# Two low-rank projections computed with one shared stationary operand for the high and low weight parts

## The chip, the core and the metric

The kernel runs on one core of a Trainium2 chip. The metric is device time in microseconds (us) for one execution. A core has five engines that run side by side, each with its own instruction order: TensorE (PE, the matrix multiplier, with a separate line for loading its stationary operand), VectorE (DVE), ScalarE (ACT), GpSimd (POOL) and SyncE (SP, which mostly issues DMAs). They wait for each other through semaphores. Matmul results go to PSUM banks and are emptied from there by ACT or DVE.

A matmul has a stationary operand (up to 128 rows by 128 columns, the weights here) and a moving operand (the same rows by 512 columns here: 512 positions of the sequence). Its sum runs over the rows.

## The reference, cut to what matters

The program is one layer of a decoder: a norm, one input projection, an RWKV-7 branch and an S5 branch, their gated merge, an output projection, and a gated MLP with a short convolution. The input is 1024 positions by 1024 channels, in float32. The change concerns two lines of the RWKV branch:

```python
p = token_shift(h @ w_in[:, :1792], mu)
r, k, v, wd, ad, gd = split(p, ...)            # 512, 512, 512, 64, 64, 128 columns
w = -softplus(-(w0 + tanh(wd) @ w2)) - 0.5     # w2: 64 x 512
a = sigmoid(a0 + ad @ a2)                      # a2: 64 x 512
g = sigmoid(gd) @ g2                           # g2: 128 x 512, this one is not changed
```

`tanh(wd) @ w2` and `ad @ a2` are the two low-rank projections: each sums over only 64 values and gives 512 channels for each of the 1024 positions.

## The kernel before, in words

**Precision.** PE multiplies in a reduced format (fp32r). Each float32 operand is therefore split into a high part, which is a cast to that format, and a low part, which is what the cast lost. A product is then three matmuls that add up in one PSUM bank: high weights by high data, high weights by low data, low weights by high data. `mm3_steps` (L161) issues these as L172, L173 and L174, and `split` (L225) makes the two parts of data: a cast on ACT (L226) and a subtraction on DVE (L227). `load_w` (L142) does the same for weights: a DMA into a tile `wf` of which there are two buffers (L155), a cast to `wh` on ACT (L156), a subtraction to `wl` on DVE (L157).

**Layout.** Data lie transposed, with channels on the 128 partitions and positions along the row, in two halves of 512 positions (`th` 0 and 1). One output tile is 128 channels by 512 positions, which is one PSUM bank. Tiles of the projections are named `gm`; there are four such banks while the S5 stage runs, two in the RWKV stage.

**The two projections.** The input projection's tile 12 holds `wd` in its rows 0 to 63 and `ad` in rows 64 to 127. `shifted` (L1078) empties it with the token shift (L1083 on ACT, then L1084 and L1086 or L1088 on DVE), `shifted_into` applies tanh to rows 0 to 63 (L1098) and splits the whole tile into two `lx` tiles (L1101, which calls L226 and L227). `lowrank` (L1106) then loads `w_lr[0]`, which is w2 in rows 0 to 63 and zeros below, does 8 outputs (2 halves of the sequence by 4 tiles of channels) with `mm3_steps`, and does the same with `w_lr[1]`, zeros in rows 0 to 63 and a2 below. Both thus multiply all 128 rows, and the zeros drop the half that does not belong. Each output goes through ACT (L1119, for w2 also L1121) to memory (L1122). `lowrank` is called once more for g2, further on.

**The order of the work.** Instructions are put in order when the program is built. `drive` (L185) is a planner with a clock of its own, `self.now`. It has *lanes*, which are generators of a stage's main work (in the first stage, which I call the S5 stage, the S5 scan and its tables; in the second, the RWKV stage, preparation, chain and output), and a *background list*, `self.fill`, of projections that may be put between them. Each step of a lane says how long it takes and how long its result needs; while no lane is ready, or the lanes have used up their credit, the planner takes the next step of the background list and advances its clock by that step's count, 0.68 for three matmuls. How far the background list has come when a lane's step is placed therefore depends on these counts.

The background list begins with `mix_in` (L1133): tile 12, then the tiles of r, k and v (`rkv`) for a quarter of the channels, mixed with the two low-rank projections: `mixed(a, b, 3)` puts one step of `b` behind every three of `a`. Then come tile 13, further r, k and v, the gates (`gate_tiles`), later the merge (`merge`, evicted at L1203 on DVE) and the output projection. In the RWKV stage the list supplies PE with work while the lanes wait for DVE. Names that occur there are: `cz` (L715) and L723, two products of the preparation; L784 to L812, the triangular inverse's work on DVE; L822, small matmuls of 32 rows that combine the inverses' blocks; L879, matmuls of 64 rows in the chain; L935, the transposes of the stage's output. At the end of each stage a *drain* does what is left of the list or of a part of it.

**Elsewhere.** `s5_setup` and what follows it (L439 to L512) makes tables on DVE while the projections begin. Behind the RWKV stage comes the MLP (from about 735 us of the span to the end), which the change does not touch.

## Time and profile before

| | |
|---|---|
| three runs | 1462.29, 1463.06, 1465.25 us, median 1463.06 |
| the profiled execution | 1461.26 us |
| its span, first to last instruction | 1459.5 us |
| granted TensorE clock, mean | 0.986 of full |
| PE busy | 1402.2 us, 96% of the span |
| DVE busy | 1087.5 us, 75% |
| ACT busy | 746.7 us, 51% |
| the two projections' evictions (L1119) | first at 78.5, last at 122.5 us |

The span in six stretches. The columns are the stretch and its length in us, then busy time of PE, PE's weight load, DVE, ACT and POOL with the number of instructions, the granted clock, the share of the DMA engines and GB/s. The first is the front, the second has the projections beside the S5 tables, the third S5 and the first half of the RWKV stage, the fourth is the middle of the RWKV stage, the fifth its end, the sixth the MLP.

```profile
0.00:80.00 80.00, 66.42 (x281) 52.08 (x282) 71.92 (x239) 56.35 (x90) 1.18 (x10) 0.98 0.59 174
80.00:280.00 200.00, 198.95 (x1047) 167.46 (x1045) 137.87 (x198) 129.54 (x228) 6.27 (x21) 1.00 0.43 137
280.00:515.00 235.00, 230.96 (x2664) 184.12 (x2665) 147.90 (x292) 106.54 (x221) 3.60 (x10) 0.99 0.39 127
515.00:600.00 85.00, 69.86 (x452) 55.93 (x451) 74.08 (x149) 52.87 (x95) 1.08 (x2) 0.91 0.58 174
600.00:735.00 135.00, 132.42 (x1580) 103.84 (x1579) 85.50 (x165) 60.62 (x116) 4.27 (x8) 0.99 0.39 125
735.00:1460.00 725.00, 703.62 (x3142) 579.51 (x3140) 570.25 (x744) 340.82 (x449) 18.50 (x29) 0.99 0.42 137
```

In a row of a timeline, as the prediction shows them, stand the start in us, the recorded duration, the engine, the line and operation, output and inputs by their names in the program, the tile of PE's array for a matmul, shapes, and the number of instructions taken together. A bracket gives how long the engine stood idle before the row and which engine's instruction ended that. Matmuls overlap in the records: what one costs is the distance from start to start, not the duration.

### The profile page before, as it was taken

To read this page: it belongs to the slowest core of one execution; us is meant where nothing else is said; L and a number is where in the kernel's file an instruction comes from. 1 tells how busy PE (TensorE), PEld (TensorE's weight loads), DVE (VectorE), ACT (ScalarE), POOL (GpSimd) and SP (SyncE) were. 2 spreads that over 40 slices of the span, in tenths; PEclk is the share of its full clock that TensorE was granted. 3 is DMA by queue.
4 is the path that set the end of the run, shared out by engine and by line. 5 is a ranking of instruction groups with operands and counts; after the bars stand their busy time and mean duration, and the time that the engine had idled before them with its cause. 6 is when DMAs were issued, how large, how long until landed. Compare 5 with 4: busy or idle time off the path is not lost. (4 is left out here: it accounts for less than half of the span.)

```text
span 1459.5 us, 23887 instructions
## 1 busy us (share of the span) xinstructions
PE 1402.2 (96%) x9156; PEld 1142.9 (78%) x9156; DVE 1087.5 (75%) x1783; ACT 746.7 (51%) x1197; POOL 34.9 (2%) x80
## 2 busy tenths in 40 slices
PE   7999999999999989899999999999999999999996
PEld 5778888878878767678788887888888887888785
DVE  8986886378327788548688898777777777597677
ACT  7667775453424564535455464454544445444451
POOL 0000000000000000000000000000000000000001
PEclk9999999999999999899999999999999999999998
DMA  7454433542413565433555543222222228934723
GB/s 221 116 190 128 144 117 108 188 146 80 139 60 110 162 193 165 138 111 116 172 195 180 158 133 122 87 83 76 75 84 87 87 73 273 328 112 144 239 79 115
DMA packets 119682, 202.04 MB, mean 138 GB/s; under 512 B 28672, under 2 KB 34944, under 8 KB 119568
## 3 DMA queue, kind: packets, MB, share of 16 engines
q1 hardware_dynamic: 113296, 182.43, 39.4%
q0 software_dynamic: 4544, 15.80, 2.9%
q10 hardware_dynamic: 1728, 2.29, 0.4%
q8 instruction: 72, 1.18, 0.3%
q14 instruction: 42, 0.34, 0.1%
HBM read 148.04 MB, written 50.33 MB: 136 GB/s over the span
## 5 line engine op out<-in xcount | busy, mean ns | idle before, releaser
L172 PE MATMUL gm<-hh,wh 128*128 128x512 f32 x672 | 276.2, 411 | 9.1 <-DVE hl L1203 4.6
L173 PE MATMUL gm<-hl,wh 128*128 128x512 f32 x672 | 264.8, 394 | 0.0
L174 PE MATMUL gm<-hh,wl 128*128 128x512 f32 x672 | 264.6, 394 | 0.0
L156 ACT CAST wh<-wf 128x512 fp32r<-128x512 f32 x171 | 105.2, 618 | 140.9 <-PE gm L173 72.5
L157 DVE TENSOR_TENSOR wl<-wf,wh 128x512 fp32r<-128x512 f32 x171 | 117.2, 688 | 76.2 <-ACT wh L156 75.6
L172 PEld LDWEIGHTS gm<-hh,wh 128*128 128x128 f32 x672 | 127.5, 190 | 41.5 <-DVE hl L1203 5.7
L174 PEld LDWEIGHTS gm<-hh,wl 128*128 128x128 f32 x672 | 127.7, 190 | 27.8
L173 PEld LDWEIGHTS gm<-hl,wh 128*128 128x128 f32 x672 | 127.8, 190 | 24.7 <-issue 1.0
L1626 PE MATMUL d<-xl,wh 128*128 128x512 f32 x308 | 120.7, 392 | 2.1 <-DVE xl L227 2.0
L1625 PE MATMUL d<-xh,wh 128*128 128x512 f32 x308 | 120.8, 392 | 2.1 <-ACT xh L226 2.1
L1627 PE MATMUL d<-xh,wl 128*128 128x512 f32 x308 | 120.6, 392 | 0.0
L1451 PE MATMUL rp<-t,h 128*128 128x512 f32 x216 | 84.4, 391 | 1.5 <-ACT p L1465 1.5
L1453 PE MATMUL rp<-t,l 128*128 128x512 f32 x216 | 84.2, 390 | 0.5 <-DVE l L227 0.5
L1452 PE MATMUL rp<-t,h 128*128 128x512 f32 x216 | 84.1, 389 | 0.0
L1626 PEld LDWEIGHTS d<-xl,wh 128*128 128x128 f32 x308 | 58.2, 189 | 15.5 <-DVE xl L227 3.4
L1625 PEld LDWEIGHTS d<-xh,wh 128*128 128x128 f32 x308 | 58.2, 189 | 14.6 <-ACT xh L226 2.4
L1627 PEld LDWEIGHTS d<-xh,wl 128*128 128x128 f32 x308 | 58.1, 189 | 12.0
L226 ACT CAST h<-r 128x1024 fp32r<-128x1024 f32 x34 | 35.8, 1054 | 61.1 <-PE rp L1452 29.6
L227 DVE TENSOR_TENSOR l<-r,h 128x1024 fp32r<-128x1024 f32 x34 | 41.6, 1225 | 29.2 <-ACT h L226 27.7
L1472 DVE SCALAR_TENSOR_TENSOR y<-zv,vecs,y 128x1023 f32<-128x1023 f32 (+1 forms) x36 | 46.1, 1281 | 8.5 <-ACT y L1470 8.5
L1465 ACT COPY p<-rp 128x512 f32<-128x512 f32 x54 | 31.0, 574 | 36.6 <-PE rp L1453 36.6
L1451 PEld LDWEIGHTS rp<-t,h 128*128 128x128 f32 x216 | 40.5, 188 | 11.1 <-ACT p L1465 2.4
(459 smaller groups left out, 3127.6 us busy)
## 6 DMA issues: line engine op xcount, KB each, us to landing
r<-in_w_up_dram SPq DMA_DIRECT2D x36, 512.0 KB, 3.6
wf<-in_w_in_dram SPq DMA_DIRECT2D x62, 256.0 KB, 3.0
st<-in_w_down_dram SPq DMA_DIRECT2D x55, 256.0 KB, 4.0
st<-ACT SPq DMA_DIRECT2D x44, 256.0 KB, 4.3
wf<-in_w_up_dram SPq DMA_DIRECT2D x36, 256.0 KB, 2.9
ACT<-y POOLq DMA_DIRECT2D x18, 512.0 KB, 2.9
GT<-ev SPq DMA_DIRECT2D x32, 256.0 KB, 2.5
wf<-in_w_br_dram SPq DMA_DIRECT2D x32, 256.0 KB, 2.6
```

What stands on the lines that cost most here:

```text
L156: nc.scalar.copy(h[:, :n], f[:, :n])
L157: nc.vector.tensor_tensor(l[:, :n], f[:, :n], h[:, :n].bitcast(F32), ALU.subtract)
L172: mm(ps, a, xh[k], start=k == 0, stop=False)
L173: mm(ps, a, xl[k], start=False, stop=False)
L174: mm(ps, b, xh[k], start=False, stop=k == n - 1)
L1451: mm(ps, wh[:, c], xh, start=first and k == 0, stop=False, skip_group_check=True)
L1452: mm(ps, wh[:, c], xl, start=False, stop=False, skip_group_check=True)
L1453: mm(ps, wl[:, c], xh, start=False, stop=k == 3, skip_group_check=True)
L1472: V.scalar_tensor_tensor(y[:, lag:], z[:, 0:1024 - lag], self.vec(nme, i), y[:, lag:], ALU.mult, ALU.add)
L1625: mm(ps, wh[:, c], xh[:, x], start=start, stop=False, skip_group_check=True)
L1626: mm(ps, wh[:, c], xl[:, x], start=False, stop=False, skip_group_check=True)
L1627: mm(ps, wl[:, c], xh[:, x], start=False, stop=stop, skip_group_check=True)
```

## The change

`lowrank_pair` takes the place of `lowrank` for the two projections. It makes one stationary operand `lw` for each: for w2 the high part in rows 0 to 63 and the low part in rows 64 to 127, for a2 the other way round. The moving operand is the high part of the data, copied into both halves of the partitions. One full matmul then gives high by high and low by high together. The third term, high weights by low data, is a matmul of 64 rows: rows 0 to 63 for w2, rows 64 to 127 for a2. The two outputs of one position (`th`, `p`) are computed together as a group: two full matmuls (L1131), then two half ones (L1133), into two banks. A group counts 0.7 on the planner's clock, and `mixed` now places one step behind every six of `rkv`. The products and the evictions are the same numbers as before, in another arrangement; the high part is made by the same cast.

The operands are made in more and smaller operations, all on 64 partitions: for the data of each half of the sequence two casts (L1101), two copies to the other half (L1103) and two subtractions (L1102), for the weights two DMAs, two casts, two subtractions and two copies (L1121 to L1124). In `lowrank_pair` these weight operations stand outside the raised priority that `load_w` gives its own. The copies of the weights' low part (L1124) are on ACT and read what DVE has subtracted.

```diff
@@ shifted_into
             if mt == 12:
                 nc.scalar.activation(y[0:64], y[0:64], AF.Tanh)
+                hi, lo = [self.lx(), self.lx()], self.lrp.tile([128, 512], F32R, name=self.nm("lo"), tag=f"lo{th}")
+                for a, sl in enumerate(HALF):
+                    nc.scalar.copy(hi[a][sl], y[sl])
+                    nc.vector.tensor_tensor(lo[sl], y[sl], hi[a][sl].bitcast(F32), ALU.subtract)
+                    nc.scalar.copy(hi[a][HALF[1 - a]], y[sl])
+                xs.append((hi, lo))
+                return
             else:
...
+    def lowrank_pair(self, xs, js):
+
+        nc = self.nc
+        mm = nc.tensor.matmul
+        f = self.wp.tile([128, 512], F32, tag="wf", name=self.nm("wf"), bufs=NWF)
+        l = self.wp.tile([128, 512], F32R, tag="wl", name=self.nm("wl"), bufs=NWL)
+        w = [self.lrp.tile([128, 512], F32R, name=self.nm("lw"), tag=f"lw{a}") for a in range(2)]
+        for a, sl in enumerate(HALF):
+            nc.sync.dma_start(f[sl], self.a["w_lr"][js[a][0]][sl])
+            nc.scalar.copy(w[a][sl], f[sl])
+            nc.vector.tensor_tensor(l[sl], f[sl], w[a][sl].bitcast(F32), ALU.subtract)
+            nc.scalar.copy(w[a][HALF[1 - a]], l[sl].bitcast(F32))
+        for th in range(2):
+            hi, lo = xs[th]
+            for p in range(4):
+                o = slice(128 * p, 128 * p + 128)
+                ps = [self.gmp() for a in range(2)]
+                for a in range(2):
+                    mm(ps[a], w[a][:, o], hi[a], start=True, stop=False)
+                for a, sl in enumerate(HALF):
+                    mm(ps[a], w[a][sl, o], lo[sl], start=False, stop=True)
+                yield 0.7
+                for a, (_, hb, dst) in enumerate(js):
+                    t = self.ev()
+                    nc.scalar.activation(t, ps[a], AF.Tanh, bias=self.hb[hb][:, p:p + 1], scale=0.5)
+                    if dst is self.TZ:
+                        nc.scalar.activation(t, t, AF.Identity, bias=self.ones1, scale=1.0)
+                    nc.sync.dma_start(dst[p][:, th * 512:th * 512 + 512], t)
...
@@ mix_in
-        yield from mixed(self.rkv(0), self.lowrank(xs[0], ((0, "w0", self.TZ), (1, "a0", self.TA))), 3)
+        yield from mixed(self.rkv(0), self.lowrank_pair(xs[0], ((0, "w0", self.TZ), (1, "a0", self.TA))), 6)
         yield from self.inproj((13, self.shifted_into(xs[1], 13)))
-        yield from mixed(self.rkv(1), self.lowrank(xs[1], ((2, None, self.TG),)), 4)
+        yield from mixed(self.rkv(1), self.lowrank(xs[1], ((2, self.TG),)), 4)
```

`lowrank`, now for g2 alone, loses its cases for the other two. The pool `lrp` for `lw` and `lo` lives beside the S5 pool.

**PE, the start of the projections.** Here `hh` and `hl` are the high and low parts of the normed input, `lx` those of tile 12, and the first `gm` is k's tile of which the `rkv` steps are done. Before:

```order
L172 MATMUL gm_1166<-hh_561,wh_1154 128x512
...
L174 MATMUL gm_1166<-hh_612,wl_1155 128x512
L172 MATMUL gm_1182<-lx_1116,wh_1176 128x512
L173 MATMUL gm_1182<-lx_1117,wh_1176 128x512
L174 MATMUL gm_1182<-lx_1116,wl_1177 128x512
L172 MATMUL gm_1166<-hh_629,wh_1154 128x512
```

And now:

```order
L174 MATMUL gm_1179<-hh_612,wl_1168 128x512
L172 MATMUL gm_1179<-hh_629,wh_1167 128x512
...
L174 MATMUL gm_1179<-hh_669,wl_1174 128x512
L1131 MATMUL gm_1210<-lx_1119,lw_1200 128x512
L1131 MATMUL gm_1211<-lx_1120,lw_1201 128x512
L1133 MATMUL gm_1210<-lo_1121,lw_1200 128x512
L1133 MATMUL gm_1211<-lo_1121,lw_1201 128x512
L172 MATMUL gm_1179<-hh_686,wh_1173 128x512
```

Nine matmuls of k's tile stood ahead of the first low-rank product, and 18 do now; a group of four rows stands where one of three stood, and half as often.

**DVE, the same place.** `lo` is the data's low part, `wl_1199` the weights', `s5ar`, `s5ai`, `pw` and `s5q` are S5 tables in the making, `ev_1145` and `ev_1153` are tile 12's second half of the sequence. Before:

```order
L469 TENSOR_TENSOR pw_1011<-s5ai,s5ar 128x32
L157 TENSOR_TENSOR wl_1269<-wf_1270,wh_1268 128x512
L1084 SCALAR_TENSOR_TENSOR ev_1145<-gm_1120,vecs,ev_1145 128x511
L1088 SCALAR_TENSOR_TENSOR ev_1145<-last,vecs,ev_1145 128x1
L227 TENSOR_TENSOR lx_1117<-ev_1111,lx_1116 128x512
L465 TENSOR_TENSOR s5ar<-pw_1005,pw_1006 128x32
```

And now:

```order
L470 TENSOR_TENSOR s5ai<-pw_1030,pw_1031 128x128
L478 TENSOR_SCALAR s5q_1036<-s5ar 64x288
L1102 TENSOR_TENSOR lo_1121<-ev_1114,lx_1119 64x512
L1102 TENSOR_TENSOR lo_1160<-ev_1153,lx_1158 64x512
L1123 TENSOR_TENSOR wl_1199<-wf_1198,lw_1200 64x512
L157 TENSOR_TENSOR wl_1271<-wf_1272,wh_1270 128x512
L1123 TENSOR_TENSOR wl_1199<-wf_1198,lw_1201 64x512
L1102 TENSOR_TENSOR lo_1121<-ev_1114,lx_1120 64x512
L1102 TENSOR_TENSOR lo_1160<-ev_1153,lx_1159 64x512
```

The subtraction for tile 12 (L227, now L1102) stood right behind the token shift of the second half; now it stands behind the S5 tables, and the weights' (L1123) with it.

**PE, behind the second attention pass of the preparation (L723).** `gm_5624` and `gm_5650` are the same gate tile, `gm_5710` is the first half of the next one, `gm_5769` is the merge's first tile (`hh_5744`, `hl_5745` are the S5 branch's output, split). Before:

```order
L172 MATMUL gm_5624<-hh_766,wh_5366 128x512
L173 MATMUL gm_5624<-hl_767,wh_5366 128x512
L174 MATMUL gm_5624<-hh_766,wl_5367 128x512
L172 MATMUL gm_5710<-hh_731,wh_5372 128x512
L173 MATMUL gm_5710<-hl_732,wh_5372 128x512
L174 MATMUL gm_5710<-hh_731,wl_5373 128x512
```

And now:

```order
L172 MATMUL gm_5650<-hh_766,wh_5314 128x512
L173 MATMUL gm_5650<-hl_767,wh_5314 128x512
L174 MATMUL gm_5650<-hh_766,wl_5315 128x512
L172 MATMUL gm_5769<-hh_5744,wh_5763 128x512
L173 MATMUL gm_5769<-hl_5745,wh_5763 128x512
L174 MATMUL gm_5769<-hh_5744,wl_5764 128x512
```

The background list is 24 matmuls further here: the half gate tile has been done earlier and the merge stands in its place. The same shift holds from the end of the S5 stage to the last drain of the RWKV stage, in which 51 `gm` matmuls are left ahead of the first one of the output projection (`mm`), where there were 75. Between the second inverse's first L784 and its last L812, DVE has 145 rows where it had 138, the seven more being rows of 128x512 of the merge. PE has 16 matmuls fewer in all.

11 lines of the change are left out of this document (3 added, 8 removed).

## The prediction

> **What bounds the kernel now.** I read the page first: the shares of the engines and the 40 slices. Then busy time by windows, to see in which stages TensorE (PE) is really full.
>
> ```profile
> span 1459.5 us, 23887 instructions
> PE 1402.2 (96%) x9156; PEld 1142.9 (78%) x9156; DVE 1087.5 (75%) x1783; ACT 746.7 (51%) x1197; POOL 34.9 (2%) x80
> ...
> PE   7999999999999989899999999999999999999996
> DVE  8986886378327788548688898777777777597677
> ```
>
> ```profile
> 160.00:200.00 40.00, 40.00 (x219) 33.83 (x218) 35.04 (x42) 29.34 (x52) 1.06 (x3) 1.00 0.43 131
> ...
> 560.00:570.00 10.00, 8.97 (x40) 7.10 (x38) 9.69 (x23) 4.21 (x7) 0.00 (x0) 1.00 0.55 179
> ...
> 680.00:690.00 10.00, 10.00 (x51) 8.25 (x50) 8.49 (x14) 7.32 (x13) 0.00 (x0) 1.00 0.32 94
> ```
>
> After the stretch come PE, weight load, DVE, ACT and POOL, then clock, DMA share and GB/s. From 80 to 500 us, and again from 600 on, PE is full and what the changed projections cost in PE time is paid one for one. Between 515 and 600 us it is DVE that is full (9.69 of 10). So three places count: the start of the projections (74 to 82 us), the projections' own matmuls, and the DVE-bound stretch, because the change advances the background list there. I read them in PE's timeline, with ACT and DVE beside it.
>
> ```profile
> 73.90 0.39 PE L174 MATMUL gm<-hh,wl 128*128 128x512 f32 x1
> 76.21 0.50 PE L172 MATMUL gm<-lx,wh 128*128 128x512 f32 x1 [1.92 <-ACT lx L226]
> 77.23 0.79 PE L173 MATMUL gm<-lx,wh 128*128 128x512 f32 x1 [0.52 <-DVE lx L227]
> 77.82 0.63 PE L174 MATMUL gm<-lx,wl 128*128 128x512 f32 x1
> ...
> 79.96 0.53 PE L173 MATMUL gm<-hl,wh 128*128 128x512 f32 x1
> 80.32 0.39 PE L174 MATMUL gm<-hh,wl 128*128 128x512 f32 x1
> 80.55 0.39 PE L172 MATMUL gm<-hh,wh 128*128 128x512 f32 x1
> ```
>
> A full 128x512 matmul is recorded with 0.39 us, but the next starts 0.23 us later (80.32 to 80.55): 0.227 us is the price of one, not 0.39. The first projection's matmul waits 1.92 us for the split of tanh, and eight matmuls start from 76.21 to 79.96, most of them 0.43 us apart. Without this PE would have done those eight in 1.8 us from 74.13 on; it is back in step at 80.32, so 4.4 us are lost here today: 2.9 idle, 1.5 slow.
>
> **Part 1: the matmuls themselves.** Two projections of 8 outputs with 3 full matmuls each are 48 slots. Now each of 8 groups has 2 full ones and 2 half ones (64 rows by 128 columns), where it had 6 full ones. If the halves run side by side a group is 3 slots, saving 3 x 0.227 = 0.68 us; one after the other, 4 slots, saving 0.45 us. But a group now changes between the full array and half of its rows, twice. This kernel's 64-row matmuls show the price:
>
> ```profile
> 406.50 0.39 PE L174 MATMUL gm<-hh,wl 128*128 128x512 f32 x1
> 406.82 0.69 PE L879 MATMUL cz<-S,ar 64*64 64x64 f32 x32
> 407.45 0.50 PE L172 MATMUL gm<-hh,wh 128*128 128x512 f32 x1
> 407.78 0.39 PE L173 MATMUL gm<-hl,wh 128*128 128x512 f32 x1
> ...
> 509.25 1.10 PE L715 MATMUL cz<-ar,bk 64*64 64x128 f32 x30 [0.17 <-DVE gr L719]
> ```
>
> Into the small tiles the step is 0.32 instead of 0.23 us (0.09 lost), the first full matmul behind them takes 0.33 (0.10 lost), and the first half will show its own weight load in the same way (another 0.1); with the drain behind the last half I take 0.35 us per group, between 0.2 (the two excesses seen alone) and 0.5. Side by side or not: 30 matmuls of 128 columns start within 1.10 us, 0.037 each, while 128 columns at the full matmul's pace are 0.227 / 4 = 0.057. So tiles in other rows do overlap, and the halves here write two different banks; I take side by side. Then 8 x (0.68 - 0.35) = **-2.6 us**; one after the other 8 x (0.45 - 0.35) = -0.8. Nothing at all, or a small loss, comes out where the change of tiles costs 0.5.
>
> The Trainium skill speaks against the halves: TensorEngine Tiling (Array Packing), Key Properties, has a change of tiling mode drain the array. The trace agrees (0.32 where 0.23 is usual). Without that rule the sum would be 8 x 0.68 = -5.4 us, with the row's price -2.6.
>
> **Part 2: 24 matmuls of the background list move.** The planner gives the front stage a fixed time and counts 0.7 for a group, where six old matmuls counted 1.36. So the list goes 24 full matmuls further before the S5 stage ends (+24 x 0.227 = +5.4 us there), and behind it every lane's matmuls stand at the same places of PE's order as before, up to the last drain, where 24 fewer are left (-5.4 us). The window at 680 shows PE full there and the one at 160 shows it full in front, so the two cancel. What remains is that between them the list is 24 matmuls ahead of the lanes: Part 4.
>
> **Part 3: the operands come later.** PE now does 18 matmuls of k's projection first, where it did 9, so it reaches the first group at 74.13 + 9 x 0.227 = 76.2 us. What it waits for has become longer. The rows of ACT and then of DVE:
>
> ```profile
> 72.63 1.28 ACT L1098 ACT_TABLE_LOAD   x1 [1.71 <-DVE ev L1084]
> 73.93 0.63 ACT L1098 ACTIVATE ev<-ev 64x512 f32<-64x512 f32 x1
> 74.46 0.60 ACT L156 CAST wh<-wf 128x512 fp32r<-128x512 f32 x1
> 74.97 0.68 ACT L1083 ACTIVATE ev<-gm,mu 128x512 f32<-128x512 f32 x1
> 75.55 0.60 ACT L226 CAST lx<-ev 128x512 fp32r<-128x512 f32 x1
> ```
>
> ```profile
> 71.21 0.68 DVE L157 TENSOR_TENSOR wl<-wf,wh 128x512 fp32r<-128x512 f32 x1
> 71.81 0.74 DVE L1084 SCALAR_TENSOR_TENSOR ev<-gm,vecs,ev 128x511 f32<-128x511 f32 x1
> ...
> 76.36 0.21 DVE L1088 SCALAR_TENSOR_TENSOR ev<-last,vecs,ev 128x1 f32<-128x1 f32 x1
> ...
> 78.60 0.22 DVE L470 TENSOR_TENSOR s5ai<-pw,pw 128x64 f32<-128x64 f32 x1
> ...
> 80.27 0.31 DVE L478 TENSOR_SCALAR s5q<-s5ar 64x288 f32<-64x288 f32 x1
> ```
>
> A cast holds ACT 0.51 us (74.46 to 74.97), L1083 0.58. In the new order the weights' L157 no longer stands ahead of L1084, so L1084 runs from 71.2; the table load and tanh follow to 73.95. Then ACT does the cast of the one half (74.5), L1083 of the second half of the sequence (75.1), three casts (76.6), its tanh (77.25), and six casts, two of them of the weights (80.3). The last two, L1124, copy the weights' low part across, so they wait for DVE. DVE takes L1084 and L1088 of the second half when ACT's L1083 is done (75.2 to 76.0), then ten S5 set-up operations that the new order puts ahead (78.60 to 80.59 is nine of them, with the tenth 2.1 us: 78.1), then two subtractions of 0.6 (79.3), the first of the weights (done at 80.0), one L157, and the second of the weights (done at 81.2). So ACT's L1124 for the first operand ends at 80.9 and for the second at 81.9, and PE starts its first group at 81.0 and goes on at 82.0. That is 4.8 + 0.8 = 5.6 us of waiting, and I add the same 1.5 us at the slow pace: 7.1 lost instead of 4.4, **+2.7 us**. Bounds: +0.5 where the casts of 64 partitions or DVE's small operations go faster than their rows, +4.5 where the slow pace lasts longer because the wait does.
>
> The slow pace is what the Trainium skill, TensorE: Matmul & The Clock Gate, Part 1, calls the gated clock, half speed after an idle window of about 3.4 us. The trace agrees in the pace (0.43 against 0.23). By that rule a wait of 4.8 us alone would be followed by one such window at half speed, an estimate of 1.7 us where I took 1.5.
>
> Behind the wait stand k's own matmuls, whose output ACT and DVE must empty before the next group's bank is free. ACT reaches it behind a cast that waits for the next weights (their buffer is freed at 81.2, and a load takes some 3 us), at about 85; PE needs the bank at about 87. I cost that at nothing; if it fails, 1 us.
>
> **Part 4: the DVE-bound stretch.** Half a gate tile (24 matmuls, gm_5710) stood between the second attention pass and the merge. Now the merge starts in its place, and at the other end two more merge tiles fall ahead of the triangular inverse's last DVE work (L812), for which PE waits:
>
> ```profile
> 522.18 0.75 DVE L227 TENSOR_TENSOR hl<-ld,hh 128x512 fp32r<-128x512 f32 x1
> ...
> 532.48 0.68 DVE L1203 SCALAR_TENSOR_TENSOR hl<-ev,gm 128x512 f32<-128x512 f32 x1
> ...
> 561.57 0.69 DVE L157 TENSOR_TENSOR wl<-wf,wh 128x512 fp32r<-128x512 f32 x1
> 562.17 0.27 DVE L795 TENSOR_TENSOR tm<-mt 128x108 f32<-128x108 f32 x1
> ```
>
> ```profile
> 533.21 0.50 PE L172 MATMUL gm<-hh,wh 128*128 128x512 f32 x1 [3.90 <-DVE hl L1203]
> ...
> 597.53 1.91 PE L822 MATMUL rp<-ld,gr 32*32 32x32 f32 x62 [2.95 <-DVE ld L812]
> ```
>
> The merge cannot start sooner than its inputs, whose fourth split ends at 522.9 (522.18 + 0.75) whatever stands ahead on PE; so PE waits at the start instead of doing the gate tile. From the inverse's first transpose to its last L812, DVE's order has 145 rows where it had 138: seven more of 128x512, each 0.60 us (561.57 to 562.17), 4.2 us. The stretch ends with PE waiting 2.95 us for L812, so DVE's delay reaches PE. Against it, the first two evictions (L1203, at 532.48 today, with 3.90 us of PE's waiting) come earlier, which gives some of it back. I take **+3.4 us**, nearer to the upper end because DVE is 97% busy; bounds -1 (the earlier evictions give back more than the two tiles cost) and +5.
>
> **The sum.** -2.6 + 2.7 + 3.4 = +3.5 us. The profiled execution took 1461.26 us (span 1459.5, and 1.8 around it), so 1464.8 for such an execution. The runs' median is 1463.06, 1.8 above the profiled one; the predicted median is 1463.06 + 3.5 = **1466.6 us**.
>
> **The rivals.**
>
> Rival A, faster: PE is the only bound. The operands come in time and DVE's extra rows lie in its own waits, so only Part 1 counts, with changes of tiles between their price and nothing (8 x 0.68 = 5.4 saved): -2.6 to -5.4, middle -4, **1459.1 us**. For it: nearly all of PE's slices read 9. Against it: PE already waits 1.92 us for a shorter chain of splits. It decides if PE's wait before the first group stays under 2 us.
>
> Rival B, no change: the operands are late, but the two extra merge tiles cost nothing, because the earlier evictions make up for them: -2.6 + 2.7, **1463.2 us**. For it: the 3.90 us wait sits just where the merge is advanced. Against it: the last wait there is for L812, which stands behind all of DVE's rows.
>
> Rival C, slower still: the halves run one after the other and DVE's seven rows count in full: -0.8 + 2.7 + 4.5, **1469.5 us**. For it: nothing in this trace is a 64-row matmul over 128 columns and 512 data columns. Against it: the 30 in 1.10 us.
>
> That the change does not do what it says (halves computed as full-width work) would show as 4 slots a group and falls together with C.
>
> **How the numbers follow.** This kernel's runs lie within 3 us of each other, so 0.2% (2.9 us, 1460.1 to 1466.0) is about what a measurement tells from no change. Chances: forecast 0.42 (own range 1464.5 to 1468.5), A 0.16, B 0.24, C 0.18. Faster: nearly all of A, 0.15. Within: B's 0.22, a piece of the forecast 0.06 and of A 0.01, 0.29. Slower: 0.36 of the forecast, 0.02 of B, C's 0.18, 0.56. The range leaves out a little under one in ten on each side, the lowest third of A and the top of C: 1458.5 to 1471.5.
>
> **What would show it.** In the changed profile: PE's wait before its first L1131 row, released by ACT's L1124, near 5 us (right) or under 2 (A). The spacing inside a group: the two L1133 rows a few ns apart (side by side) or 0.2 us apart (C), and about 0.33 us to the full matmul behind. The start of the first small matmul of the second inverse's L822 against the rest of the timeline, and the wait for L812: later by the sum of what came ahead plus 3 to 4 us (right) or by no more than what came ahead (B). From the last L935 group to the first mm row: 5.4 us shorter. If that last piece is not shorter, because merge inputs are then late, the time is above the range.

## The result, and the profile after

The changed kernel is slower. Its median is 1485.47 us (1482.13 to 1486.55), beside 1462.67 us for the kernel before on the same chip: a ratio of 1.0156 with a 95% interval of 1.0131 to 1.0180, some 22.8 us. The prediction was 1466.6 us with a range of 1458.5 to 1471.5, so the sign was right and the size wrong by 19 us.

The page of the changed kernel, the lines that answer to those shown of before:

```profile
span 1484.2 us, 23854 instructions
PE 1414.0 (95%) x9140; PEld 1146.0 (77%) x9140; DVE 1088.2 (73%) x1785; ACT 748.7 (50%) x1203; POOL 34.9 (2%) x80
...
PE   7989999899999889799999999999999999999996
DVE  8985885377425878646697798777777777698677
```

PE has 16 matmuls fewer and is busy for longer (1414.0 us against 1402.2), because more of them ran at the slow pace; and it shows more and deeper dips. To place the loss I set the start of the same instruction in both traces side by side. The rows of the table are instructions that mark the stages; the last column is how much longer the stretch up to that row has become.

| up to | before, us | after, us | stretch before | stretch after | longer by |
|---|---|---|---|---|---|
| last L614 row, end of the S5 stage's products | 265.7 | 275.7 | 265.7 | 275.7 | 10.0 |
| first L879, the first chain | 392.6 | 411.0 | 126.9 | 135.4 | 8.5 |
| last L723, second attention pass | 510.3 | 531.0 | 117.7 | 120.0 | 2.3 |
| L832 of the second inverse, its level step | 602.2 | 631.6 | 92.0 | 100.6 | 8.7 |
| first L935 of the second output | 679.7 | 708.7 | 77.4 | 77.0 | -0.4 |
| first `mm` row of the output projection | 709.9 | 733.5 | 30.2 | 24.8 | -5.4 |
| end of the span | 1459.5 | 1484.2 | 749.6 | 750.7 | 1.1 |

The 24 matmuls of the background list that moved are in it twice: about 5.4 of the first 10.0 us, and the -5.4 us near the end. What is left is a loss in four places. PE's waits from 60 to 760 us, grouped, first before and then after (what waited and for what, us in total, times, longest):

```profile
PE gm L172 <- DVE hl L1203: 4.6, 2, 3.9
PE gm L172 <- DVE ev L1203: 3.1, 2, 2.2
```

```profile
PE gm L172 <- DVE ev L1234: 6.2, 3, 2.6
PE gm L173 <- DVE hl L227: 5.9, 6, 2.0
PE gm L1131 <- ACT lw L1124: 5.8, 1, 5.8
PE gm L172 <- ACT wh L156: 5.6, 1, 5.6
```

The wait for L1124, at the start of the projections, was foreseen. The one for L156 was not in the prediction at all, and those for L1234 (the merge's evictions, L1203 before) and for L227 (the splits of its inputs) are the middle of the RWKV stage.

**The start.** PE, then ACT and DVE in the changed kernel:

```profile
76.43 0.39 PE L174 MATMUL gm<-hh,wl 128*128 128x512 f32 x1
82.66 1.43 PE L1131 MATMUL gm<-lx,lw 128*128 128x512 f32 x2 [5.85 <-ACT lw L1124]
84.03 0.79 PE L1133 MATMUL gm<-lo,lw 64*128 64x512 f32 x2
84.75 0.79 PE L172 MATMUL gm<-hh,wh 128*128 128x512 f32 x1
...
89.53 0.40 PE L174 MATMUL gm<-hh,wl 128*128 128x512 f32 x1
...
102.50 0.61 PE L1131 MATMUL gm<-lx,lw 128*128 128x512 f32 x2
103.04 0.50 PE L1133 MATMUL gm<-lo,lw 64*128 64x512 f32 x2
103.48 0.50 PE L172 MATMUL gm<-hh,wh 128*128 128x512 f32 x1
103.81 0.39 PE L173 MATMUL gm<-hl,wh 128*128 128x512 f32 x1
```

```profile
79.55 1.26 ACT L1122 CAST lw<-wf 64x512 fp32r<-64x512 f32 x2
80.72 0.61 ACT L1101 CAST lx<-ev 64x512 fp32r<-64x512 f32 x1
81.35 0.62 ACT L1103 CAST lx<-ev 64x512 fp32r<-64x512 f32 x1
81.99 1.26 ACT L1124 CAST lw<-wl 64x512 fp32r<-64x512 f32 x2
```

```profile
80.20 0.68 DVE L1123 TENSOR_TENSOR wl<-wf,lw 64x512 fp32r<-64x512 f32 x1
```

PE reaches the first group at 76.66 (76.43 and a pitch of 0.23), gets its operands at 82.6, and then works at the half pace until 89.5. That pace is the granted clock: the row of this stretch shows 0.50 (third number from the end), where the mean of the execution is 0.976.

```profile
82.66:89.00 6.34, 6.34 (x14) 4.24 (x15) 4.95 (x13) 2.50 (x5) 0.00 (x0) 0.50 0.45 143
```

From 76.66 to the first S5 table product (L542) at 119.36 it does seven groups and 108 full matmuls; at 0.98 us a group, 0.227 a matmul and 0.10 for the matmul behind each of six groups that is 32.0 us, and it took 42.7. So 10.7 us are lost there, where the kernel before lost 4.4.

**The end of the S5 stage.** PE and SP's DMA issues, before and then after:

```profile
269.15 0.50 PE L172 MATMUL gm<-hh,wh 128*128 128x512 f32 x1 [1.05 <-ACT ev L1158]
```

```profile
269.12 0.32 SPq L1159 DMA_DIRECT2D GT<-ev  x1
269.82 0.82 SPq L155 DMA_DIRECT2D wf<-in_w_in_dram  x2
```

```profile
283.70 0.79 PE L172 MATMUL gm<-hh,wh 128*128 128x512 f32 x1 [5.59 <-ACT wh L156]
```

```profile
278.86 0.32 SPq L1190 DMA_DIRECT2D GT<-ev  x1
279.93 0.81 SPq L155 DMA_DIRECT2D wf<-in_w_in_dram  x2
```

In both kernels the next gate tile's weights are asked for only when the next stage begins, right behind the store of a gate half tile (GT). Before, the background list was then in the middle of a gate tile: the second half, 24 matmuls with weights already at hand, covered the load. After the move by 24 the tile is finished, and the very next matmul needs the new weights.

**The middle.** Engines' busy time from the second attention pass to the level step, before and after (columns as in the table of stretches above), and then what DVE waited for in the stretch after:

```profile
510.28:602.23 91.95, 76.81 (x475) 60.49 (x472) 77.15 (x154) 53.71 (x96) 1.08 (x2) 0.91 0.59 178
```

```profile
531.00:631.63 100.63, 82.61 (x476) 62.84 (x472) 79.51 (x158) 55.51 (x98) 1.08 (x2) 0.88 0.54 161
```

```profile
DVE wl L157 <- ACT wh L156: 7.3, 7, 2.0
```

DVE's work in it grew by 2.4 us (77.15 to 79.51), but the stretch by 8.7: DVE was idle for 21.1 us instead of 14.8. Of this, 7.3 us in seven pieces are waits for the merge's weights, which ACT casts only when PE has let go of older ones (ACT's waits for PE at this cast, L156, are 14.7 us in the stretch, 5.9 before); before there was one such wait of DVE, of 1.2 us. The loss stands clear of the scatter between kernels: in the profiled executions of the six kernels below that keep the list in its place (e1, e3, e9, e10, e12, e15) this stretch took 86.7 to 92.4 us, in those that have it 24 matmuls ahead there (e2, e4, e5, e11) 96.4 to 102.8.

### The profile page after: what moved, and what is told of

The parts are those of the page before. It is cut to its first block, busy times and chain, and to the rows that moved or that the text cites. A ratio compares the mean times of both kernels' runs of the same rounds, so it can differ in the third digit from the quotient of the medians.

```text
span 1484.2 us, 23854 instructions
## 1 busy us (share of the span) xinstructions
PE 1414.0 (95%) x9140; PEld 1146.0 (77%) x9140; DVE 1088.2 (73%) x1785; ACT 748.7 (50%) x1203; POOL 34.9 (2%) x80
## 5 line engine op out<-in xcount | busy, mean ns | idle before, releaser
L172 PE MATMUL gm<-hh,wh 128*128 128x512 f32 x672 | 281.0, 418 | 14.8 <-DVE ev L1234 6.2
L173 PE MATMUL gm<-hl,wh 128*128 128x512 f32 x672 | 269.5, 401 | 5.9 <-DVE hl L227 5.9
L174 PE MATMUL gm<-hh,wl 128*128 128x512 f32 x672 | 268.5, 400 | 0.0
L157 DVE TENSOR_TENSOR wl<-wf,wh 128x512 fp32r<-128x512 f32 x169 | 115.7, 687 | 101.9 <-ACT wh L156 80.3
L156 ACT CAST wh<-wf 128x512 fp32r<-128x512 f32 x169 | 104.3, 619 | 156.8 <-PE gm L173 87.7
L227 DVE TENSOR_TENSOR l<-r,h 128x1024 fp32r<-128x1024 f32 x34 | 41.6, 1224 | 29.2 <-ACT h L226 27.7
L1482 PEld LDWEIGHTS rp<-t,h 128*128 128x128 f32 x216 | 40.6, 188 | 10.9 <-ACT p L1496 2.4
```

Source lines behind the costliest of these rows:

```text
L156: nc.scalar.copy(h[:, :n], f[:, :n])
L157: nc.vector.tensor_tensor(l[:, :n], f[:, :n], h[:, :n].bitcast(F32), ALU.subtract)
L172: mm(ps, a, xh[k], start=k == 0, stop=False)
L173: mm(ps, a, xl[k], start=False, stop=False)
L174: mm(ps, b, xh[k], start=False, stop=k == n - 1)
L1482: mm(ps, wh[:, c], xh, start=first and k == 0, stop=False, skip_group_check=True)
```

## Experiments: what the place of the background list costs

Theory P says that most of the loss has nothing to do with the products: the planner's smaller count for a group moved the background list, and its new place is bad at two points. Its rival S says that the late start hands its delay on. Two kernels part them, one with the new products and the list in its old place, one with the old products and the list moved.

The first, e1, has two counted steps per group, so that TensorE's order is that of before with four products in place of six:

```diff
+                yield 0.68
                 ps = [self.gmp() for a in range(2)]
...
-                yield 0.7
+                yield 0.68
...
-(1, "a0", self.TA))), 6)
+(1, "a0", self.TA))), 3)
```

> The change as it is, but each group of four products counts two steps of 0.68 on the planner's clock, so that the background list stands in TensorE's order exactly where it stood before the change; the products and the way the operands are made are those of the change. Theory P (the place of the background list makes most of the loss: it moved the end of the S5 stage to the end of a gate tile, 5.6 us of waiting for the next weights and 1.8 us at the slow pace, and the merge to a place where its inputs are late): the changed median 1485.5 less 5 to 6 at the end of the S5 stage, about 10 in the middle of the RWKV stage and perhaps the 4 of the stall near 406 us: 1466 to 1471, with only the start of the projections (5.9 us of waiting) left. Theory S (the late start itself carries on through the program, by shifted transfers and clock): within 3 us of 1485.

Measured: 1463.44 us, ratio to before 1.0006 (0.9990 to 1.0022), below the expectation. The wait at the first group is there unchanged (5.85 us, for L1124), and the end of the S5 stage's products comes 3.2 us later than before; but the stretch in the middle is 89.1 us, 2.9 less than before, which makes up for it. Why it is shorter is not settled.

The second, e2, is the kernel before, and only the count is changed:

```diff
-                    yield from self.mm3_steps(ps, w, p, [xs[th][0]], [xs[th][1]])
+                    for _ in self.mm3_steps(ps, w, p, [xs[th][0]], [xs[th][1]]):
+                        yield 0.68 if hb is None else 0.35
```

> The kernel before, in which a step of the two low-rank projections counts 0.35 instead of 0.68 on the planner's clock, so that the background list runs 24 matmuls further, as in the change; products and operands are those of before. Theory P: the wait at the end of the S5 stage and the losses in the middle of the RWKV stage come without any change of the products: 1463 + 5.5 + 10 = 1478, up to 1483 if the stall near 406 us belongs to it. Theory S: 1463, within 3 us.

Measured: 1478.77 us, ratio 1.0106 (1.0086 to 1.0126). At the end of the S5 stage stands the new wait, and the stretch in the middle is 99.8 us:

```profile
279.63 0.79 PE L172 MATMUL gm<-hh,wh 128*128 128x512 f32 x1 [5.88 <-ACT wh L156]
```

So the count alone, 0.35 for 0.68, costs the old kernel 16.8 us, and the change without it costs nothing that can be measured. Theory S falls. The two do not add up to the 22.8 us of the change: some 5 us are missing, of which the shorter middle of e1 is a part.

Next, e5 takes the first of the two points by itself. TensorE's order stays that of the change; the weights of the next gate tile are loaded and split before the S5 stage ends:

```diff
-        ws = [self.load_w(self.a["w_in"][mt]) for mt, _ in jobs]
+        ws = [self.pre.pop(mt, None) or self.load_w(self.a["w_in"][mt]) for mt, _ in jobs]
+        self.gate_at = jobs[-1][0] + 1
...
                 self.drain(lambda: self.mixed_in and not self.open)
+                self.pre[self.gate_at] = self.load_w(self.a["w_in"][self.gate_at])
```

> The change as it is, TensorE's order untouched, but the weights of the next gate tile are loaded and split before the S5 stage ends instead of behind the store of the last gate tile. If the 5.6 us of waiting there are for these weights alone: the wait is gone, 1485.5 - 5.6 - 1.8 = about 1478. If something else holds TensorE there (the next stage's buffers, ACT's work for the preparation): the wait stays under another name and the time within 2 us of 1485.

Measured: 1478.15 us, ratio 1.0094 (1.0067 to 1.0120), 7.3 us less than the change. The wait is gone; what is left there is one for an eviction:

```profile
277.66 0.50 PE L173 MATMUL gm<-hh,wh 128*128 128x512 f32 x1 [0.78 <-ACT ev L1191]
```

Two runs then moved the list by a whole gate tile. In e6 each of a group's two steps counts 1.36, in e7 nothing; else they are e1.

> The products and operands of the change with each group counting 2.72 on the planner's clock, so that the background list stands 48 matmuls (a whole gate tile, not half of one) behind its old place. Theory P: the S5 stage ends in the middle of a tile again, so no wait for weights there (under 1.5 us); before the merge one more gate tile stands as cover. Like the run with the list in its old place, 1461 to 1465; lower by up to 4 if the old cover was too short. If any move of the list costs (rival), 1470 or more.

> The same with groups that count nothing, so that the list stands 48 matmuls ahead of its old place. Theory P in its two parts: a whole tile keeps the end of the S5 stage in the middle of a tile, so the wait of 5.6 us there is absent; but the merge comes earlier still, before its inputs, so the loss in the middle of the RWKV stage is there and not smaller than in the change: 1472 to 1480. If the loss at the end of the S5 stage came from the list being ahead and not from the place inside the tile, the wait is there too: 1480 or more. If the middle's loss were only the seven more rows of the merge on DVE, twice as many: about 1470.

Measured: e6 1488.44 us (1.0178; 1.0153 to 1.0204), e7 1488.21 us (1.0166; 1.0131 to 1.0201). The first point came out as said: with a whole tile neither has the wait of 5.6 us at the end of the S5 stage; in e6 the longest there is 1.72 us, in e7 it is the small one for an eviction:

```profile
282.06 0.50 PE L172 MATMUL gm<-hh,wh 128*128 128x512 f32 x1 [0.78 <-ACT ev L1190]
...
533.28 0.80 PE L172 MATMUL gm<-hh,wh 128*128 128x512 f32 x1 [12.43 <-ACT hh L226]
```

The second row is where e7 went above its expectation: a whole tile earlier, the merge stands before its inputs for 12.43 us. In e6 the expectation was wrong. Its middle was the shortest of the three (86.6 us), but the merge, now later, ran into the second chain, and its evictions came late (the row below); from the level step to the output projection it took 135.8 us where before took 107.7, 10.9 of them for the 48 matmuls moved there:

```profile
684.07 0.77 PE L172 MATMUL gm<-hh,wh 128*128 128x512 f32 x1 [7.14 <-DVE hl L1235]
```

So the list's old place is not one side of a slope: later costs as well as earlier.

In e8 the preloaded weights of e5 stay, and the list falls back to its old place before the second preparation:

```diff
-        yield from self.inproj(*((18 + m, lambda th, ps, m=m: use(m, th, ps)) for m in ms))
+        for i, c in enumerate(self.inproj(*((18 + m, lambda th, ps, m=m: use(m, th, ps)) for m in ms))):
+            yield 2 * c if ms[0] == 8 and i < 8 else c
```

> The run with the preloaded weights, and in addition eight steps of a gate tile in the RWKV stage count double, so that the list falls back to its old place before the second preparation; from there on TensorE's order is that of the run with the list kept. If the loss in the middle is the place of the merge, it goes: 1478 less 8 to 10, 1468 to 1470, or 1464 if the stall near 406 us goes as well. If it was something that the early part of the program hands on (shifted transfers), it stays: 1476 to 1479.

Measured: 1461.23 us, ratio 0.9997 (0.9979 to 1.0014), below the expectation, with 89.3 us in the middle where e5 had 102.8. The whole loss is undone with the late start still in it (5.84 us of waiting at the first group).

Two runs ask what makes the middle's loss. In e11 the four tiles that the merge first reads come from memory written long before. (They are the RWKV branch's output, `YR`, and so are `hh_5744` and `hl_5745` in the order shown ahead of the prediction, which calls them the S5 branch's.)

```diff
-                self.nc.sync.dma_start(self.yr[k], self.YR[k])
+                self.nc.sync.dma_start(self.yr[k], self.TG[k][:, 0:512])
```

> The change as it is, TensorE's order untouched, but the four tiles of the RWKV branch that the first merge reads come from g's projection, which has long been in memory, and not from the output stage that has just stored them (so the merged values are not the reference's). From the end of the second attention pass to the level step of the inverse the kernel before takes 92.0 us, the change 100.6. If that loss is the merge standing where its inputs are not there yet, the waits for their splits (1.8 and 2.0 us and the slow pace behind them) go and the stretch takes 91 to 94: 1485.5 less 7 to 9, 1477 to 1479. If it is the added rows of the merge on DVE, or a lack of PE work later in the stretch, it stays at 99 to 101: 1483 to 1486.

Measured: 1480.63 us, ratio 1.0116 (1.0098 to 1.0135), 4.8 us less than the change, and 96.4 us in the stretch, between the two expectations. But the edit did not make the first inputs early. Their loads stand at the same place in the order of the DMAs, and the first landed as late as in the change. ACT's cast of it, in the change and then in e11:

```profile
534.21 0.62 ACT L226 CAST hh<-ld 128x512 fp32r<-128x512 f32 x1 [5.13 <-DMA ld<-YR]
```

```profile
534.33 0.62 ACT L226 CAST hh<-ld 128x512 fp32r<-128x512 f32 x1 [4.64 <-DMA ld<-TG]
```

Only the third and the fourth landed sooner (at 536.3 and 538.4 us, in the change at 538.9 and 539.6). PE's waits for the splits did not go; the longer of two, whose split now stands behind a transpose on DVE (L784, 2.12 us) and no longer waits for the transfer:

```profile
540.30 0.78 PE L173 MATMUL gm<-hl,wh 128*128 128x512 f32 x1 [2.02 <-DVE hl L227]
```

So e11 does not tell what the lateness of the inputs costs.

In e14 the change is left as it is up to the first output, and the list falls back only there (the diff of e8 with tile 13 in place of 8, without the preload), so that the half gate tile stands again between the second attention pass and the merge.

> The change as it is up to the stage's first output; there eight steps of the second last gate tile count double, so that the list falls back by 24 matmuls between the first output and the second attention pass, and the half gate tile stands again between that pass and the merge. Everything ahead of it (late start, wait for weights at the end of the S5 stage, stall near 406 us) stays. If the merge's place alone makes the loss in the middle, the stretch from the second attention pass to the level step falls from 100.6 to 89 to 92 us and what follows it stays, 1485.5 - 9 to 14 = 1471 to 1476. If the loss was handed on from ahead (transfers and buffers late by then), the stretch stays at 98 or more and the time at 1483 to 1486.

Measured: 1475.79 us, ratio 1.0091 (1.0064 to 1.0118), 9.7 us less than the change. The stretch is 87.0 us, and DVE's waits for the merge's weights are down to one of 1.2 us, as before:

```profile
528.50:615.50 87.00, 74.79 (x474) 59.15 (x471) 75.34 (x152) 53.80 (x96) 1.08 (x2) 0.93 0.61 178
```

Not all 13.6 us of the stretch (100.6 to 87.0) reach the end. The 24 matmuls are taken from in front of the second attention pass, but little of their 5.4 us came back there (528.5 against 531.0, and 0.9 of these 2.5 us stood already at the first output), since PE then waited 4.85 us for the first output's DVE work; and behind the stretch they are done after all (108.1 us from the level step to the output projection, 101.8 in the change). So the middle's loss is the merge's place and is not handed on from ahead: up to the first output everything was within 1 us of the change.

## Experiments: the group of products and the late start

The second half product is left out in e4:

```diff
-                    mm(ps[a], w[a][:, o], hi[a], start=True, stop=False)
-                for a, sl in enumerate(HALF):
+                    mm(ps[a], w[a][:, o], hi[a], start=True, stop=a == 1)
+                for a, sl in enumerate(HALF[:1]):
                     mm(ps[a], w[a][sl, o], lo[sl], start=False, stop=True)
```

> The change as it is, without the second of the two half products of each group (so a2's projection lacks its third term). In the changed kernel a group takes 0.98 us from its first product to the next full matmul (102.50 to 103.48), and that matmul 0.33 instead of 0.23. If the two halves run side by side, one of them takes as long as both and the group stays at 0.95 to 1.0 us. If they run one after the other at 0.22 each, it falls to 0.74 to 0.80.

Measured, in a single execution (1483.60 us): the group takes 0.97 us (101.96 to 102.93) with one half and 0.98 with two. In the changed kernel the records of the two halves start 4 ns apart (103.044 and 103.048). The halves run side by side, and the second is free.

```profile
101.96 0.61 PE L1131 MATMUL gm<-lx,lw 128*128 128x512 f32 x2
102.50 0.50 PE L1133 MATMUL gm<-lo,lw 64*128 64x512 f32 x1
102.93 0.50 PE L172 MATMUL gm<-hh,wh 128*128 128x512 f32 x1
```

For the start, e3 puts the first group of e1 further back (four counted steps ahead of it, and later groups in pairs), and e9 further still, with the groups spread evenly; both keep the list. The core of e9, as a difference to e1:

```diff
-                yield 0.68
+                for _ in range(9 if p == th == 0 else 1):
+                    yield 0.45333
                 ps = [self.gmp() for a in range(2)]
...
-(1, "a0", self.TA))), 3)
+(1, "a0", self.TA))), 2)
```

> As the run before last (list kept in its place), and the first group of the two projections is put behind 15 steps of k's and r's projections (45 matmuls) instead of 6 (18 matmuls). If the wait of 5.9 us at the first group is for operands that are merely late, it goes, and with it the slow pace behind it: 8 us less than the run with the list kept, and since the kernel before loses 4.4 us at that place, below it: 1456 to 1460. If the wait only moves (to the next weights of the background list, or to banks that ACT has not emptied), within 3 us of the run with the list kept, 1465 to 1471.

> The run with the list kept in its place, with the first group behind 18 steps of the other projections (54 matmuls) and one group after every four steps, so that the operands are there and ACT has time to empty two banks per group. If lateness of the operands and of the evictions is all that was lost at the start: neither the 5.9 us wait nor the 2.6 us one of the late groups, 1456 to 1459, faster than the kernel before. If the wait moves to something else again: 1461 to 1463.

Measured: e3 1461.63 us (0.9985; 0.9964 to 1.0006), between its two expectations. The wait for the operands fell from 5.85 to 0.42 us, but the second group followed closely, and ACT had not emptied the banks:

```profile
89.36 1.09 PE L1133 MATMUL gm<-lx,lw 128*128 128x512 f32 x2 [2.60 <-ACT ev L1139]
```

With the groups spread, e9 measured 1453.79 us, ratio 0.9941 (0.9918 to 0.9964): faster than the kernel before and than expected, and the best of all that were run. The largest wait left up to the end of the S5 stage's products is one of 0.87 us at 95.17, again for ACT's eviction (L1139).

How much of this is the new products and how much the late start? In e15 the kernel before, with its own products, starts them as late:

```diff
-        for j, hb, dst in js:
+        for _ in range(8 if len(js) > 1 else 0):
+            yield 0.45333
+        for j, hb, dst in js:
```

(its steps of these projections count 0.45333, and `mixed` places one behind every two.)

> The kernel before with its own products and operands, in which the two projections start behind 18 steps (54 matmuls) and then take one step after every two, as in the run with the groups spread; the list keeps its place. The run with the groups spread was 8.8 us faster than before. If that is the start freed of its wait (before loses 4.4 us there) plus the products (about 2.2 us, by 8 groups of 1.08 us where 8 x 1.36 stood), this run shows the start alone: 1457 to 1459. If the products make more of it than their sum says, 1461 to 1463; if the late start makes all of it, 1454 to 1456.

Measured: 1460.73 us, ratio 0.9984 (0.9969 to 0.9998), between the expectations. The end of the S5 stage's products lies at 262.5 us in e15 and at 261.3 in e9, against 265.7 before: 3.2 us from the late start, 1.2 more with the new products. The rest of e9's gain, about half of its 8.8 us, is not in the start. In its profiled execution, the fastest of its six, the stretch in the middle took 86.7 us, where before took 92.0 and e15 92.4; why it did is not settled, with the order of the list the same there.

In e10 (e1) and e12 (e9) the copies to the other half of the partitions are on GpSimd, which has only a few memsets to do there:

```diff
-                    nc.scalar.copy(hi[a][HALF[1 - a]], y[sl])
+                    nc.gpsimd.tensor_copy(hi[a][HALF[1 - a]], y[sl])
...
-            nc.scalar.copy(w[a][HALF[1 - a]], l[sl].bitcast(F32))
+            nc.gpsimd.tensor_copy(w[a][HALF[1 - a]], l[sl].bitcast(F32))
```

> The run with the list kept in its place, and the six copies to the other half of the partitions (four of the data, two of the weights' low part) are made by GpSimd instead of ACT. If the first group waits for ACT's row of small operations, 12 of them of 0.63 us where 2 casts of data and 2 of weights stood, taking six away shortens the wait from 5.9 us by 3 to 4: about 2 us, 1459 to 1461. If it waits for DVE's subtractions (the weights' second one ended at 82.1 in the change), the wait falls by less than 1 us and the time stays at 1462 to 1464.

> The last two together: groups spread and late, copies on GpSimd. If the start is clean without GpSimd's help already, the same as the spread run within 1 us; if ACT's load still holds evictions up there, 1 to 3 us less. Either way 1455 to 1459.

Measured: e10 1467.59 us (1.0040; 1.0024 to 1.0056), e12 1460.26 us (0.9975; 0.9959 to 0.9991), both above their expectations. Taking six operations off ACT did not shorten the wait at all:

```profile
82.74 0.79 PE L1132 MATMUL gm<-lx,lw 128*128 128x512 f32 x1 [5.90 <-POOL lw L1124]
```

```profile
84.01 1.01 POOL L1124 CAST lw<-wl 64x512 fp32r<-64x512 f32 x1 [1.33 <-DVE wl L1123]
```

GpSimd's copy waited for DVE's subtraction and took 1.01 us where ACT's took 0.63, so the first operand was no earlier and the second later. But this does not show that ACT's row is harmless, because the run slowed DVE as well. Beside GpSimd's operations (three copies and a memset) four of DVE's S5 set-up rows took 0.63, 0.70, 0.71 and 1.03 us, where the same rows took 0.22, 0.28, 0.29 and 0.31 in e1: 2.0 us more ahead of the weights' subtraction. The third of the four, in e1 and then in e10, where a copy L1103 ran on GpSimd from 78.12 to 78.88:

```profile
78.58 0.29 DVE L475 COPY s5q<-s5ar 64x288 f32<-64x288 f32 x1
```

```profile
78.33 0.71 DVE L475 COPY s5q<-s5ar 64x288 f32<-64x288 f32 x1
```

In the change itself the copy L1124 stood ready to go at 80.88, when the subtraction had ended, and began at 81.99, behind the last casts of ACT's row. What a shorter row alone would give is not shown. That e10 is 4 us slower than e1, and e12 6 us slower than e9 at the same order on PE, is more than this explains, and is left open.

## Why the prediction was wrong, step by step

**Part 1, the matmuls: right.** A group takes 0.98 us and the matmul behind it 0.33 instead of 0.23, so 1.08 us for what took 1.36. That is 0.28 saved per group and 2.2 in all, where the prediction said 2.6. The halves side by side are 3 slots (0.68 us), so the changes of tiles cost 0.40 per group, where 0.35 was taken. The draining that the Trainium skill names (TensorEngine Tiling (Array Packing), Key Properties) is thus seen here too, at that price.

**Part 2, "the two cancel": the step that failed first.** The 24 matmuls themselves did cancel (30.2 to 24.8 us behind the second output). But from "every lane's matmuls stand at the same places of PE's order" it does not follow that nothing is lost between. The list is not a stream of equal matmuls: its tiles have weights to be loaded, and the end of a stage falls somewhere in a tile. A move by half a tile took the cover from a load (5.59 us of waiting and 1.8 us at the slow pace, 1.05 us of waiting before). The trace of before showed it: the load is issued at 269.82, behind the last store, and the 24 matmuls that started at 269.15 hid it. I had the move of exactly half a tile in front of me and did not ask where the stage's end fell. The sum had no term for it, that is 0 us; taken out alone, in e5, it is 7.3 us.

**Part 3, the late operands: right in kind, mis-sized.** The wait was 5.85 us where 5.6 (4.8 and 0.8) was worked out, and L1124 the releaser that was named. That the two are so close is in part luck. The prediction had L1124 wait for DVE's subtraction, but this was done at 80.88, and L1124 began at 81.99, behind ACT's own row: its casts of 64 partitions follow each other by 0.63 us, not by the 0.51 that was taken from a cast of 128, so the row ended at 81.97 and not at 80.3. The larger error was the slow pace. It was taken over as 1.5 us from before; it lasted from 82.66 to 89.5 and cost 1.1 in the first group and 2.2 in the matmuls behind it. A late eviction at the third group (0.29 us of waiting, and 1.43 us to the next full matmul instead of 0.98) came on top. The loss against before was 6.3 us at the start (10.7 less 4.4), with 2.7 predicted and an upper bound of 4.5. The rule of the Trainium skill that the prediction quoted (TensorE: Matmul & The Clock Gate, Part 1), with its estimate of 1.7 us, was too small in the same way; and the window of about 3.4 us that it names is no threshold here, since the half pace also followed waits of 1.92 us (before) and 2.58 us (after).

**Part 4, the DVE-bound stretch: right place, wrong mechanism, and less than half the size.** The prediction had 3.4 us, the stretch is 8.7 longer. I counted seven more rows of DVE, 4.2 us, and wrote off the gate tile's cover as an exchange of work for waiting. DVE's busy time grew by 2.4 us only, and its idle time by 6.3. In this stretch DVE is not a bound that fills itself: its order alternates the inverse with the merge's splits, and each of these waits for ACT, which waits for PE, which waits for DVE. A merge that starts in want of its inputs slows all three. That the place of the merge makes it, e14 shows (100.6 to 87.0 us). How much of it is the lateness of the inputs is not known, since in e11, the one run on it, the first input was as late as in the change. The alternation of the three engines is argued from the waits and not shown by a run.

**What was not foreseen.** At 404 us PE stood still for 1.49 us in the midst of a group of small matmuls, with no releaser, and worked at the slow pace for 5 us behind it; before had a pause of 0.26 us there:

```profile
405.99 0.72 PE L832 MATMUL cz<-gr,ld 32*32 32x32 f32 x33 [1.49 <-issue]
...
408.18 0.80 PE L172 MATMUL gm<-hh,wh 128*128 128x512 f32 x1
```

With the new wait (5.59 us, 1.8 of pace, less the 1.05 before) it makes up the 8.5 us of that stretch: some 2 us fall to the pause, an estimate by what is left over. Pauses of 0.45 to 1.26 us stand there in e1, e5, e8 and e14, and none in e9 and e15; no run was made for their cause.

**The rivals and the range.** Rival A fell with the wait of 5.85 us, B with the middle, C with the halves side by side (its sum also took 4.5 us for the seven rows that Part 4 counts at 4.2). None of them had the list's place as its mechanism, and the largest of them ended at 1469.5. The bounds were added up from the costs that I had seen, and the range left no room for one that I had not.

## What to carry to other kernels

Where a planner sets the order by counted times, a change of a count is a change of the program: compare, for every stage's end and every hand-over, what the moved background work covered there and which loads stand behind it, before costing the work itself. A wait of some us on PE can cost more than itself, since the pace behind it can be halved for several us. And a cheaper product whose operands take longer to prepare wants a later place: here the same products lost 1.6% or gained 0.6% by where they and the list were put, though only about half of that gain is accounted for.

## What the runs showed of the hardware that I had not expected

Two matmuls of 64 rows by 128 columns, in different halves of the rows and into two banks, take no longer than one (0.98 and 0.97 us for the group). PE went to the half pace, a granted clock of 0.50, not only behind the long waits: 2.58 us of waiting were enough in the changed kernel (1.92 and 0.52 before, as the prediction shows), and the pace held until 598.1. Behind the wait of 1.05 us at 269.15 it stayed at 0.23 us a matmul.

```profile
594.38 0.58 PE L172 MATMUL gm<-hh,wh 128*128 128x512 f32 x1 [2.58 <-DVE ev L1234]
```

From 60 to 760 us there are 37 matmuls of the projections before, and 85 after, behind which the next one starts 0.35 to 1 us later without a wait between. Their excess over 0.227 us adds up to 8.7 us before and to 19.7 after, and PE's waits of 0.3 us and more to 24.4 and 36.7: of the 24.7 us by which the span grew, some 11 are pace and 12 are waits. A third thing showed by the way: DVE's L475 beside a copy on GpSimd took 0.71 us (e10), without one 0.29 (e1).
